# Softmax weights normalised by a product with diag(1/sum) on TensorE, in all attentions of a two-block transformer kernel

## The chip, the cores and the metric

The program runs on one core of a Trainium2 chip. The metric is the device time of one execution in microseconds (us); a kernel's figure is the median of its runs. A core has TensorE (PE in the rows, with PEld for its weight loads), VectorE (DVE), ScalarE (ACT), GpSimd (POOL) and SyncE (SP, which issues nearly all weight transfers here).

## The reference, cut to what matters

Two transformer blocks run after each other on 256 tokens of width 1024, all in float32. The first has two layers with a context stream beside the latent one, each layer with grouped attention, a Hyena convolution branch, a merge and a gated feed-forward. The second has one layer: a convolution branch and dilated attention, a memory cross-attention, and a mixture of 32 experts. Four kinds of attention occur, and all end in the same few lines:

```
s = jnp.einsum('bqhgd,bkhd->bhgqk', q_blk, keys) * scale
p = jax.nn.softmax(s, axis=-1)            # exp(s - max) / sum
out = jnp.einsum('bhgqk,bkhd->bqhgd', p, vals)
```

Before `p` can be multiplied with the values it must be divided by its row sums and turned, since TensorE sums over partitions: queries lie on the partitions of `p`, and keys must.

## The kernel before, in words

The kernel splits most float32 operands into a high part and a low part (`divide`: ScalarE writes the rounded high part, VectorE subtracts it for the low part) and multiplies them in three products (`mm3`). Weights come through `Stream`: SyncE loads pieces of 128x1024 into tiles `u`, the two halves are made from them, and the loads are issued some pieces ahead. Tiles `u` are 4 KB a partition, and there are NSLOT = 46 of them. Tiles `t` (2 KB, NTMP = 12) hold intermediate results; small columns are `s`; `ps` are the 8 banks that TensorE writes to.

The program's order is set as it is recorded, by a planner. Generators (projections, Hyena, attention) yield what they wait for; `drive` and `tick` step whichever can go on, by the estimates in `Timer`, which charges each instruction to its engine: for a TensorE product, n/2400 us times 4 for float32, or times 2 for a transposition, with a least of 0.107 us. Work whose operands are late by that estimate is put off by `defer`, and background work on VectorE (`modulation_sums`, products of 128x1024 with a column) is fed in between. All engines then run their queues in the recorded order. Each instruction is recorded through one helper, so nearly every row has line L289 (L290 in the changed kernel), and tiles must be told by name.

An attention of the first block goes by units of four heads: `scores` writes the scores of two heads to `ps`, `softmax` takes the row maximum on VectorE and the exponential on ScalarE, which leaves the row sums in `sm`. Its deferred `rest` takes the reciprocal, and multiplies the 128x512 or 128x256 exponentials in place by it (`times`: on ScalarE or VectorE, whichever the planner holds free first). Then `turn` transposes four heads at a time into one bank, a 128x128 block each, and `divide` splits what comes out. The other attentions have the same steps for pairs of 128x256: `softmax_pair`, where ScalarE does the multiplication, and `turn_probs`.

By units, layer 0 has 12 `turn` pairs of 4 blocks with 8 transpositions each, layer 1 has 8, the dilated attention 6, and the memory attention 4 groups of 4: 96 + 64 + 48 + 16 = 224 transpositions of exponentials. 112 other transpositions of `t` tiles stay as they are.

Two other places hold float32 products of the form that the change brings in. `leave` (the end of the memory attention) adds a residual 128x128 block of float32, as the stationary operand, times the identity `ident` into `acc`, by a plain `matmul` (not a transposition). And `route` begins with a loop over `range(self.WARM)`, WARM = 24, of plain products `ident` by `ident`.

Of the kernel before, what the change touches and what calls it, by code (L numbers as in the profile page):

```python
# [11 lines left out]
F32 = mybir.dt.float32  # L12
# [15 lines left out]
NE = 32  # L28
CAP = 32
EFF = 512  # L30
NSLOT = 46
NTMP = 12

# [160 lines left out]
class Part:  # L196
# [1 line left out]


    def __init__(self, ap, n=1):  # L200
        self.ap, self.left, self.eta = ap, n, None

    def __getitem__(self, key):
        return self.ap[key]
# [9 lines left out]
class Timer:  # L214
# [12 lines left out]
    def issue(self, engine, op, aps, kw):  # L227
        outs = [aps[0]] + ([kw["accum_out"]] if kw.get("accum_out") is not None else [])
        ins = aps[1:] + [v for k, v in kw.items() if k != "accum_out" and isinstance(v, bass.AP)]
        size = max(int(np.prod(a.shape[1:])) for a in aps)  # L230
        if op == "dma_start":
            engine = "DMA"
            start, cost = max(self.free["DMA"], self.free["PE"]), int(np.prod(aps[0].shape)) * 4 / 360e3
        else:
            start = self.free[engine]
            if engine == "PE":
                n = int(np.prod(aps[0].shape[1:]))
                slow = aps[-1].dtype == F32
                cost = n / 2400 * (2 if op == "transpose" else 4 if slow else 1)
                if "tile_position" in kw:  # L240
                    cost /= 4
                cost = max(cost, self.LEAST if slow else 0.03) + self.EACH
            else:
                cost = self.FIX[engine] + size * self.PER[engine]
        for a in ins:
            t, e = self.wrote.get(a.name, (0.0, engine))
            start = max(start, t + (self.LAG if e != engine else 0.0))
        for a in outs:
            t, e = self.wrote.get(a.name, (0.0, engine))
            if e != engine:  # L250
                start = max(start, t + self.LAG)
            t, e = self.read.get(a.name, (0.0, engine))
            if e != engine:
                start = max(start, t + self.LAG)
        end = start + cost
        self.free[engine] = end
        late = self.LATE if engine == "DMA" else 0.0
        for a in ins:
            if self.read.get(a.name, (0.0, engine))[0] <= end:
                self.read[a.name] = (end, engine)  # L260
        for a in outs:
            self.wrote[a.name] = (end + late, engine)

    def there(self, x):
        if isinstance(x, float):
            return x
        if isinstance(x, Part):
            if x.ready:
                return self.there(x.ap)
            return FAR if x.eta is None else x.eta  # L270
        if not isinstance(x, bass.AP):
            return x() if isinstance(x, types.FunctionType) else 0.0
        return self.wrote.get(x.name, (0.0, ""))[0] + self.LAG
# [145 lines left out]
class Net:  # L419
# [662 lines left out]
    def softmax(self, ps, n, scale):  # L1082

        nc = self.nc
        m, nb, sm, rs = ([self.small(1) for _ in ps] for _ in range(4))
        P = [Part(self.tmp()) for _ in ps]
        for i, p in enumerate(ps):
            nc.vector.tensor_reduce(m[i], p[:, :n], axis=AX, op=OP.max)
        for i, p in enumerate(ps):
            nc.vector.scalar_tensor_tensor(nb[i], m[i], -1.0, scale[i], op0=OP.mult, op1=OP.mult)  # L1090
        for i, p in enumerate(ps):
            nc.scalar.activation(P[i][:, :n], p[:, :n], AF.Exp, bias=nb[i], scale=scale[i], accum_out=sm[i])

        def rest(i):
            nc.vector.reciprocal(rs[i], sm[i])
            self.times(P[i][:, :n], P[i][:, :n], rs[i])
            P[i].done()
        for i in range(len(ps)):
            if not self.dry:
                P[i].eta = self.timer.there(sm[i]) + 0.8  # L1100
            self.defer(lambda i=i: rest(i), sm[i])
        return P

    def times(self, out, x, col):

# [6 lines left out]
    def attention(self, kT, V, Q, R, units):  # L1112

        nc = self.nc

        def scores(u, hs):
            g, i, k0, nk = u
            q = slice(i * 128, (i + 1) * 128)
            n = nk * 128
            ks = slice(k0 * 128, k0 * 128 + n)  # L1120
            ps = [self.ps() for _ in hs]
            for hh, p in zip(hs, ps):
                hd = 4 * g + hh
                self.need(Q[hd])
                self.need(kT[g])
                self.mm3(p[:, :n], Q[hd][:, 0, q], Q[hd][:, 1, q], kT[g][:, 0, ks], kT[g][:, 1, ks], True, True)
            return self.softmax(ps, n, [R[4 * g + hh][:, i:i + 1] for hh in hs])

        def turn(P, kt):
            ps = self.ps()  # L1130
            for hh in range(4):
                self.need(P[hh])
                self.transpose(ps[:, hh * 128:(hh + 1) * 128], P[hh][:, kt * 128:(kt + 1) * 128])
            o = Part(self.u([128, 2, 512], F32R))
            self.divide([(o[:, 0], o[:, 1], ps)], [o])
            return o

        def values(u, ps, part, kt):
            g, i, k0, nk = u
            gs = slice(g * 128, (g + 1) * 128)  # L1140
            v = V[k0 + kt]
            self.need(v)
            self.need(part)
            self.mm3(ps, v[:, 0, gs], v[:, 1, gs], part[:, 0], part[:, 1], kt == 0, kt == nk - 1)

        def finish(u, ps):
            g, i = u[:2]
            q = slice(i * 128, (i + 1) * 128)
            o = [Q[4 * g + hh] for hh in range(4)]
            self.divide([(o[hh][:, 0, q], o[hh][:, 1, q], ps[:, hh * 128:(hh + 1) * 128]) for hh in range(4)])  # L1150

        def score_steps(u, hs):
            g = u[0]
            while len(kT) <= g or any(4 * g + hh not in R or not self.known(Q[4 * g + hh]) for hh in hs) or \
                    not self.known(kT[g]):
                yield BLOCK
            yield (kT[g], *[x for hh in hs for x in (Q[4 * g + hh], R[4 * g + hh])])
            return scores(u, hs)

        last = None  # L1160
        for u in units + [None]:
            P = []
            if u:
                P += yield from score_steps(u, (0, 1))
            if last:
                v, PP = last
                yield PP
                PT = [turn(PP, kt) for kt in range(2)]
            if u:
                P += yield from score_steps(u, (2, 3))  # L1170
            if last:
                yield PT
                ps = self.ps()
                for kt in range(2):
                    values(v, ps, PT[kt], kt)
                if v[3] > 2:
                    PT = [turn(PP, kt) for kt in range(2, 4)]
                    yield PT
                    for kt in range(2, 4):
                        values(v, ps, PT[kt - 2], kt)  # L1180
                finish(v, ps)
            last = [u, P]
# [497 lines left out]

    def softmax_pair(self, ps, scale=None):

        nc = self.nc
        m, nb, sm, rs = (self.small(2) for _ in range(4))
        P = Part(self.tmps(SEQ)[0])
        if scale is None:
            nc.vector.tensor_reduce(nb, ps, axis=AX, op=OP.max, negate=True)
        else:
            nc.vector.tensor_reduce(m, ps, axis=AX, op=OP.max)
            nc.vector.scalar_tensor_tensor(nb, m, -1.0, scale, op0=OP.mult, op1=OP.mult)  # L1690
        for i in range(2):
            nc.scalar.activation(P[:, i], ps[:, i], AF.Exp, bias=nb[:, i:i + 1],
                                 scale=1.0 if scale is None else scale[:, i:i + 1],
                                 accum_out=sm[:, i:i + 1])

        def rest():
            nc.vector.reciprocal(rs, sm)
            for i in range(2):
                nc.scalar.activation(P[:, i], P[:, i], AF.Copy, scale=rs[:, i:i + 1])
            P.done()  # L1700
        if not self.dry:
            P.eta = self.timer.there(sm) + 0.8
        self.defer(rest, sm)
        return P

    def turn_probs(self, P, o=None):
# [2 lines left out]
        pt = self.ps().rearrange("p (k q) -> p k q", k=2)  # L1709
        for k in range(2):  # L1710
            for i in range(2):
                self.transpose(pt[:, k, i * 128:(i + 1) * 128], P[:, i, k * 128:(k + 1) * 128])
        if o is not None:
            self.nc.scalar.activation(o, pt, AF.Copy)
            return Part(o, 0)
# [701 lines left out]
```

## Time and profile before

| | |
|---|---|
| median of 3 runs | 2033.67 us (2031.07 to 2033.98) |
| profiled execution | 2032.56 us, of it 2030.8 us span from the first instruction to the last |
| mean granted TensorE clock | 0.987 |
| TensorE busy | 1914.3 us, 94% of the span |
| VectorE, ScalarE busy | 1080.7 us (53%), 711.9 us (35%) |

Busy time is an average over stages. By stretches of 50 us TensorE is busy for 45 us or more until about 1550 us, mostly 49 to 50; from about 1600 us on, in the experts, it is busy for 42 to 46 us and waits for weights, while the DMA engines move 407 to 409 GB/s. A matmul row's duration counts from its start to its modelled end, and these overlap; the cost of one in a dense stretch is the distance between starts. A plain float32 product leaves two records in the trace and two weight loads, a transposition one of each.

### The profile page before, as it was taken

The numbers are of one execution on the slowest core, as the hardware profiler recorded it, in microseconds if no ns is written. First come the engines' busy times: TensorE is split into PE (matmuls) and PEld (weight loads), VectorE is DVE, ScalarE is ACT, GpSimd is POOL, SyncE is SP. The second block draws the span as 40 slices with busy tenths as digits, with TensorE's granted clock in tenths as the row PEclk, the third lists the DMA queues.
The fourth block names the chain that finished last, engine by engine and source line by source line (L and its number), as shares of the span: only waits on it lengthen the run. The fifth ranks groups of instructions, "written<-read, shape, count | busy, mean of one in ns | idle before, by whom it ended". The sixth has DMA issues, their size and how long they took to land. (4 is left out here: it accounts for less than half of the span.)

```text
span 2030.8 us, 27948 instructions
## 1 busy us (share of the span) xinstructions
PE 1914.3 (94%) x11155; PEld 1444.2 (71%) x11155; DVE 1080.7 (53%) x1747; ACT 711.9 (35%) x1164; POOL 41.4 (2%) x49
## 2 busy tenths in 40 slices
PE   7999999999999999999999999999999898888886
PEld 3788888887878888899889999998888431111111
DVE  6988997376763343588877655578564210000001
ACT  3433664244322222364654544346652100000001
POOL 0000000000000000000000000000100000000000
PEclk9999999999999999999999999999999999999998
DMA  9434145443553242455267465553378999999997
GB/s 373 171 113 130 57 127 175 147 134 99 158 156 104 83 125 73 150 172 162 89 237 275 159 188 177 181 164 93 114 245 313 405 407 409 409 409 409 409 410 301
DMA packets 121437, 432.10 MB, mean 213 GB/s; under 512 B 13654, under 2 KB 14152, under 8 KB 121304
## 3 DMA queue, kind: packets, MB, share of 16 engines
q1 hardware_dynamic: 119464, 424.64, 58.8%
q0 software_dynamic: 1696, 5.38, 0.9%
q8 instruction: 89, 1.46, 0.3%
q14 instruction: 44, 0.36, 0.1%
q10 hardware_dynamic: 144, 0.26, 0.0%
HBM read 428.13 MB, written 2.10 MB: 212 GB/s over the span
## 5 line engine op out<-in xcount | busy, mean ns | idle before, releaser
L289 PE MATMUL ps<-u 128*128 128x256 f32 (+3 forms) x9088 | 1583.7, 346 | 46.5 <-DVE u L289 20.8
L289 PEld LDWEIGHTS ps<-u 128*128 128x128 f32 (+2 forms) x9088 | 1291.7, 187 | 329.3 <-DMA u<-w 105.2
L289 DVE TENSOR_TENSOR u<-u 128x1024 fp32r<-128x1024 f32 (+4 forms) x414 | 432.2, 1071 | 208.3 <-ACT u L289 197.0
L289 ACT ACTIVATE u<-u 128x1024 fp32r<-128x1024 f32 (+2 forms) x392 | 359.7, 961 | 269.7 <-DVE u L289 176.8
L289 PE MATMUL ps<-u,t 128*32 128x512 f32 (+1 forms) x1028 | 213.4, 618 | 33.3 <-DMA u<-w 21.1
L289 PEld LDWEIGHTS ps<-u,t 128*32 128x32 f32 (+1 forms) x1028 | 43.7, 111 | 186.5 <-DMA u<-w 115.7
L289 ACT ACTIVATE u<-ps 128x512 fp32r<-128x512 f32 (+3 forms) x201 | 88.8, 496 | 221.8 <-PE ps L289 220.2
L289 DVE TENSOR_TENSOR t<-t,ps 128x512 f32<-128x512 f32 x12 | 8.2, 686 | 255.2 <-PE ps L289 240.1
L289 DVE SCALAR_TENSOR_TENSOR u<-u,cs 128x1024 f32<-128x1024 f32 x112 | 139.9, 1278 | 0.1
L289 ACT ACTIVATE t<-ps 128x512 f32<-128x512 f32 (+1 forms) x62 | 36.5, 596 | 279.5 <-PE ps L289 279.3
L289 DVE TENSOR_TENSOR u<-u,ps 128x512 f32<-128x512 f32 x53 | 36.2, 686 | 101.4 <-PE ps L289 101.4
L289 DVE SCALAR_TENSOR_TENSOR u<-ps,mod,u 128x256 f32<-128x256 f32 x96 | 41.9, 478 | 72.8 <-PE ps L289 72.8
L289 DVE SCALAR_TENSOR_TENSOR u<-ps,s,u 128x512 fp32r<-128x512 f32 (+2 forms) x24 | 15.4, 662 | 115.9 <-ACT u L289 96.1
L289 ACT ACTIVATE u<-t 128x512 fp32r<-128x512 f32 (+1 forms) x74 | 41.8, 592 | 89.8 <-DVE t L289 84.4
L289 DVE TENSOR_TENSOR u<-ps,u 128x512 fp32r<-128x512 f32 (+2 forms) x135 | 59.4, 489 | 23.2 <-ACT u L289 16.3
L289 ACT ACTIVATE u<-ps,s 128x512 fp32r<-128x512 f32 (+1 forms) x26 | 15.9, 646 | 152.6 <-PE ps L289 149.0
L289 POOL TENSOR_TENSOR s<-s,mhalf 128x4 f32<-128x4 f32 (+2 forms) x25 | 30.2, 1206 | 1687.6 <-DVE s L289 1679.5
L289 ACT ACTIVATE t<-ps,s 128x256 f32<-128x256 f32 (+1 forms) x80 | 49.2, 629 | 40.6 <-DVE s L289 40.5
L289 PE MATMUL ps<-ident,t 128*128 128x128 f32 (+1 forms) x352 | 50.5, 278 | 9.3 <-DVE t L289 7.2
L289 PEld LDWEIGHTS ps<-ident,t 128*128 128x128 f32 (+1 forms) x352 | 40.3, 143 | 24.0 <-DVE t L289 14.7
L289 ACT ACTIVATE t<-u 128x512 f32<-128x512 f32 x41 | 25.3, 629 | 77.1 <-DVE u L289 76.8
L289 DVE TENSOR_TENSOR u<-t,u 128x512 fp32r<-128x512 f32 (+1 forms) x74 | 44.2, 642 | 2.6 <-ACT u L289 2.6
(132 smaller groups left out, 688.3 us busy)
## 6 DMA issues: line engine op xcount, KB each, us to landing
u<-w SPq DMA_DIRECT2D x381, 512.0 KB, 10.2
u<-w_in SPq DMA_DIRECT2D x102, 512.0 KB, 4.1
u<-w_mod SPq DMA_DIRECT2D x96, 512.0 KB, 4.8
u<-w_gu SPq DMA_DIRECT2D x88, 512.0 KB, 3.7
u<-w_dn SPq DMA_DIRECT2D x32, 512.0 KB, 3.6
u<-w_out SPq DMA_DIRECT2D x24, 512.0 KB, 4.4
u<-w_oa SPq DMA_DIRECT2D x16, 512.0 KB, 4.8
u<-w_dn SPq DMA_DIRECT2D x16, 384.0 KB, 3.2
```

Of the source, the lines that this page charges most:

```text
L289: return fn(*args, **kw)
```

## The change

The multiplication of the exponentials is dropped. `rest` builds instead a diagonal matrix `dg` of 128x128 from the identity times the reciprocal column (`diagonal`, by `times`, so on ScalarE or VectorE), and `turn` and `turn_probs` multiply: the exponentials are the stationary operand as before, but the moving one is the diagonal in place of the identity, and the instruction is a plain float32 matmul in place of a transposition. The eight `dg` tiles of 512 B take the room of one `u` tile: NSLOT goes from 46 to 45. In the planner, a TensorE product of 128 columns is charged like a transposition (times 2), and an attention weight counts as there once its diagonals are.

```
-NSLOT = 46
+NSLOT = 45
+NDIAG = 8
...
-                cost = n / 2400 * (2 if op == "transpose" else 4 if slow else 1)
+                cost = n / 2400 * (2 if op == "transpose" or n == 128 else 4 if slow else 1)
...
         def rest(i):
             nc.vector.reciprocal(rs[i], sm[i])
-            self.times(P[i][:, :n], P[i][:, :n], rs[i])
+            P[i].scales.append(self.diagonal(rs[i]))
             P[i].done()
...
+    def diagonal(self, col):
+        d = self.wp.tile([128, 128], F32, name="dg", tag="dg", bufs=NDIAG)
+        self.times(d, self.ident, col)
+        return d
...
-                self.transpose(ps[:, hh * 128:(hh + 1) * 128], P[hh][:, kt * 128:(kt + 1) * 128])
+                self.nc.tensor.matmul(ps[:, hh * 128:(hh + 1) * 128], P[hh][:, kt * 128:(kt + 1) * 128],
+                                      P[hh].scales[0], start=True, stop=True)
...
-            for i in range(2):
-                nc.scalar.activation(P[:, i], P[:, i], AF.Copy, scale=rs[:, i:i + 1])
+            P.scales += [self.diagonal(rs[:, i:i + 1]) for i in range(2)]
...
-                self.transpose(pt[:, k, i * 128:(i + 1) * 128], P[:, i, k * 128:(k + 1) * 128])
+                self.nc.tensor.matmul(pt[:, k, i * 128:(i + 1) * 128], P[:, i, k * 128:(k + 1) * 128], P.scales[i],
+                                      start=True, stop=True)
```

On TensorE, in the attention of layer 0 (`ps<-ident,t` are transpositions of exponentials, `ps<-u` products of split operands, `ps<-ones_87,t` row sums), there stands before:

```order
L289 MATMUL ps<-ident,t 128x128 x8
L289 MATMUL ps<-u 128x512 x6
L289 MATMUL ps<-ones_87,t 128x1 x8
L289 MATMUL ps<-u 128x512 x30
L289 MATMUL ps<-ident,t 128x128 x8
L289 MATMUL ps<-u 128x512 x30
L289 MATMUL ps<-u 128x256 x6
```

And now, at the same place (`ps<-dg,t` are the products with a diagonal):

```order
L290 MATMUL ps<-dg,t 128x128 x8
L290 MATMUL ps<-ones_87,t 128x1 x8
L290 MATMUL ps<-u 128x512 x36
L290 MATMUL ps<-dg,t 128x128 x8
L290 MATMUL ps<-u 128x512 x30
L290 MATMUL ps<-ones_87,t 128x1 x8
L290 MATMUL ps<-u 128x512 x24
L290 MATMUL ps<-u 128x256 x6
```

Each group of 8 transpositions has become 8 products at nearly the same place among the same work; row sums move by 6 to 24 products. Over the whole program 224 instructions change so, and the number of matmul instructions of each other form stays the same.

On ScalarE, at the start of the dilated attention (`t,s<-ps,s` are exponentials, `t<-t,s` their multiplication), there stands before:

```order
L289 ACTIVATE t,s<-ps,s 128x256 x4
L289 ACTIVATE u<-ps,s 128x256 x2
L289 ACTIVATE t<-t,s 128x256 x4
L289 ACTIVATE t,s<-ps,s 128x256 x4
L289 ACTIVATE t<-t,s 128x256 x4
L289 ACTIVATE u<-u 128x1024
L289 ACTIVATE u<-ps 128x512 x2
```

And now:

```order
L290 ACTIVATE t,s<-ps,s 128x256 x4
L290 ACTIVATE u<-ps,s 128x256 x2
L290 ACTIVATE t,s<-ps,s 128x256 x4
L290 ACTIVATE dg<-ident,s 128x128 x2
L290 ACTIVATE u<-ps 128x512 x2
L290 ACTIVATE u<-u 128x1024 x2
```

Of eight multiplications here, two diagonals stay on ScalarE and six go to VectorE. Over the program, 50 multiplications on ScalarE and 30 on VectorE become 22 diagonals on ScalarE and 58 on VectorE, and ScalarE switches its function table 20 times where it did 18 times.

## Rows read from the trace of the kernel before

**Rows 1.** Page, part 1: busy us of each engine, share, instructions.
```profile
PE 1914.3 (94%) x11155; PEld 1444.2 (71%) x11155; DVE 1080.7 (53%) x1747; ACT 711.9 (35%) x1164; POOL 41.4 (2%) x49
```
**Rows 2.** Stretches of the four attentions: length, then busy us, clock, DMA share, GB/s.
```profile
215.00:340.00 125.00, 124.45 (x645) 103.51 (x644) 112.32 (x246) 79.82 (x174) 3.28 (x2) 1.00 0.41 129
986.00:1056.00 70.00, 65.13 (x464) 59.27 (x462) 55.75 (x114) 46.39 (x90) 2.02 (x2) 1.00 0.44 145
1372.00:1452.00 80.00, 75.47 (x563) 64.34 (x563) 60.50 (x126) 56.24 (x132) 2.25 (x2) 0.98 0.29 91
1500.00:1530.00 30.00, 27.27 (x216) 26.86 (x215) 18.29 (x28) 19.27 (x40) 0.00 (x0) 0.94 0.72 248
```
**Rows 3.** Timeline of PE, layer 0: start us, duration, what, records.
```profile
248.97 7.77 PE L289 MATMUL ps<-u 128*128 128x512 f32 x36
256.58 1.03 PE L289 MATMUL ps<-ident,t 128*128 128x128 f32 x8
257.37 9.15 PE L289 MATMUL ps<-u 128*128 128x256 f32 x42
```
**Rows 4.** Timeline of PE at the end of the memory attention.
```profile
1540.93 1.14 PE L289 MATMUL ps<-ident,u 128*128 128x128 f32 x8
1541.90 0.98 PE L289 MATMUL ps<-t,u 128*128 128x36 f32 x8
...
1551.23 0.95 PE L289 MATMUL ps<-ones,acc 128*128 128x1 f32 x8
1552.04 4.55 PE L289 MATMUL ps<-u 128*128 128x256 f32 x36
```
**Rows 5.** The loop of WARM products on PE: records, busy us, mean ns.
```profile
L289 PE MATMUL ps<-ident 128*128 128x128 f32 x48 | 7.0, 317 | 0.0
```
**Rows 6.** Timeline of PE, memory attention: one group of four transpositions.
```profile
1505.03 0.60 PE L289 MATMUL ps<-ident,t 128*128 128x128 f32 x4
1505.38 6.00 PE L289 MATMUL ps<-u 128*128 128x256 f32 x48
```
**Rows 7.** Groups on DVE and ACT by form: busy us, mean ns, idle before.
```profile
L289 DVE TENSOR_TENSOR u<-ps,u 128x128 fp32r<-128x128 f32 x64 | 14.0, 281 | 1.7 <-ACT u L289 1.7
L289 DVE TENSOR_SCALAR t<-t,s 128x512 f32<-128x512 f32 x19 | 9.3, 487 | 0.7
L289 DVE TENSOR_SCALAR t<-t,s 128x256 f32<-128x256 f32 x14 | 4.9, 354 | 1.2 <-POOL s L289 0.8
...
L289 ACT ACT_TABLE_LOAD x18 | 23.1, 1283 | 4.9 <-DMA cols<-cols 4.6
L289 ACT ACTIVATE t<-t,s 128x256 f32<-128x256 f32 x37 | 16.8, 524 | 3.2 <-DVE s L289 3.2
L289 ACT ACTIVATE t<-t,s 128x512 f32<-128x512 f32 x13 | 9.4, 726 | 4.6 <-DVE s L289 4.6
L289 ACT ACTIVATE identr<-ident 128x128 fp32r<-128x128 f32 x1 | 0.3, 292 | 0.0
```
**Rows 8.** Waits of PE, layer 1, then dilated attention: us in total, times, longest.
```profile
PE ps L289 <- DVE u L289: 5.5, 3, 2.4
...
PE ps L289 <- ACT t L289: 4.1, 4, 1.6
```
**Rows 9.** Timeline, dilated attention: two waits of PE and what ScalarE did.
```profile
1405.53 0.73 PE L289 MATMUL ps<-u,identr 128*128 128x512 f32 x2 [1.62 <-ACT t L289]
...
1440.45 0.93 ACT L289 ACTIVATE t<-t,s 128x256 f32<-128x256 f32 x2
1441.04 0.94 PE L289 MATMUL ps<-ident,t 128*128 128x128 f32 x4 [0.96 <-ACT t L289]
```
**Rows 10.** SP's waits, 1450 to 1600 us; then a stretch of the experts, as rows 2.
```profile
SPq L289 <- PE ps L289: 75.2, 33, 14.7
...
1950.00:2000.00 50.00, 42.98 (x166) 8.99 (x166) 2.19 (x3) 1.97 (x3) 0.00 (x0) 1.00 1.03 409
```
**Rows 11.** Costliest group of VectorE's background products.
```profile
L289 DVE SCALAR_TENSOR_TENSOR u<-u,cs 128x1024 f32<-128x1024 f32 x112 | 139.9, 1278 | 0.1
```

More of the change, by code (lines that the diff above doesn't have):

```diff
@@ L200, in __init__ @@
     def __init__(self, ap, n=1):
-        self.ap, self.left, self.eta = ap, n, None
+        self.ap, self.left, self.eta, self.scales = ap, n, None, []
     def __getitem__(self, key):
@@ L268, in there @@
             if x.ready:
-                return self.there(x.ap)
+                return max(map(self.there, [x.ap, *x.scales]))
             return FAR if x.eta is None else x.eta
@@ L1102, in softmax @@
         return P
+    def diagonal(self, col):
+        if self.dry:
+            return None
+        d = self.wp.tile([128, 128], F32, name="dg", tag="dg", bufs=NDIAG)
+        self.times(d, self.ident, col)
+        return d
     def times(self, out, x, col):
```

## The prediction

> **What bounds the kernel now.** I read the page's busy shares first. TensorE is busy for 94% of the span, VectorE for 53%, ScalarE for 35% [rows 1]; the reader is to see that no other engine comes near. A share is a mean over stages, so next I cut out the four stretches with attention in them [rows 2]. In layer 0 TensorE is busy for 124.45 of 125 us at a granted clock of 1.00; in layer 1 for 65.13 of 70; in the dilated attention for 75.47 of 80; in the memory attention for 27.27 of 30. It idles there for 0.55 + 4.87 + 4.53 + 2.73 = 12.7 us in all. VectorE has 12.7 us of its own to spare in layer 0, ScalarE 45.2. So TensorE is the bound in all four, almost without slack in the first. Busy is not the same as dense, since the rows overlap; distances between starts tell. In layer 0, 36 split products of 512 columns and 8 transpositions follow each other without a gap: 7.61 us from start to start for the 36, or 0.211 each [rows 3]. TensorE runs as tightly as it does anywhere, and what is added to it there is added to the time.
>
> Whether a delay before the experts reaches the end is the second question. The experts are bound by transfers at 409 GB/s with the DMA engines' share at 1.03 [rows 10]. But those transfers start when buffers come free: between 1450 and 1600 us SyncE waits 75.2 us for TensorE to release tiles [rows 10]. All attentions lie ahead of it, so a TensorE that is later by X lets the stream start later by X.
>
> **The change on TensorE.** 224 transpositions become 224 plain float32 products of the same size: 96 in layer 0, 64 in layer 1, 48 in the dilated attention (26 groups of 8 together) and 16 in the memory attention (4 groups of 4).
>
> A group of 8 transpositions takes 257.37 - 256.58 = 0.79 us, 0.099 each [rows 3]; a group of 4 takes 0.35 [rows 6].
>
> The new form has a twin in the trace. A plain float32 product of a 128x128 block with 128 columns of the identity stands at the end of the memory attention: 8 records from 1540.93 to 1541.90, 0.97 us [rows 4]. Those are 4 products, for a plain float32 product leaves two records and two weight loads: the WARM loop of 24 products has 48 [rows 5]. So one costs 0.243 us against 0.099. As a lower bound I take float32 products with one column, which have almost nothing to stream: 8 records, 4 products, from 1551.23 to 1552.04, 0.81 us or 0.203 each [rows 4]. I take 0.243, since it is the same form; the lower bound stays for the range.
>
> A group of 8 then takes 1.94 us, 1.15 more than now; a group of 4 takes 0.97, 0.62 more. Layer 0: 12 x 1.15 = 13.8 us. Layer 1: 8 x 1.15 = 9.2. Dilated: 6 x 1.15 = 6.9. Memory: 4 x 0.62 = 2.5. Sum: 32.4 us. By the lower bound a group of 8 takes 0.83 more and one of 4 takes 0.46 more: 26 x 0.83 + 4 x 0.46 = 23.4 us.
>
> The rows thus show the plain product at 2.4 times the transposition. The Trainium skill says the same without a figure: its page "Perfetto Trace Analysis", section "Transposes", wants a logical transposition done as a transposition and not as a standard matmul, because the transposing form skips the arithmetic; the trace agrees, with 0.243 against 0.099 us. Its page "FP8 and Floating Point Precision", section "TensorE Precision Notes", gives a true float32 product four passes through the array; with the 53.3 ns for 128 columns at 2.4 GHz of the page "TensorE: Matmul & The Clock Gate", that makes an estimate of 0.213 us a product, and the sum by it would be 224 x 0.213 less the 21.9 us of the transpositions now, 25.8 us in place of 32.4.
>
> The planner charges the new product 0.107 us, like the transposition. That changes the order but no duration: groups stand where they stood, among the same products. TensorE will be later than the planner thinks, which makes operands early rather than late.
>
> **The change on ScalarE and VectorE.** ScalarE loses 50 multiplications, 16.8 + 9.4 = 26.2 us [rows 7], and gains 22 diagonals, at 0.292 us by the one copy of 128x128 from SBUF [rows 7]: 6.4 us. VectorE loses 19 of 0.487 and 11 of 0.354 us, 13.1 us, and gains 58 diagonals. A 128x128 scaling does not show on VectorE; below, it can't cost less than nothing; above, the 128x128 subtraction from PSUM takes 0.281 [rows 7]. I take the upper end, to which it is nearest in size: 16.3 us, 3 us more than before, spread over four stages with more than that to spare. Two more loads of ScalarE's table at 1.283 us [rows 7] lie on an engine that is free for a third of layer 0; if that cover fails they cost 2.6 us.
>
> So ScalarE is relieved by about 17 us net, and where does TensorE wait for it? In the dilated attention, 4.1 us in all [rows 8]. One wait of 0.96 us ends on a pair of multiplications: they run from 1440.45 for 0.93 us, and the transposition starts at 1441.04 once the first is done [rows 9]. The longest, 1.62 us, ends before a product with the mask, ahead of the softmax [rows 9]: it waits for a bank to be read by an exponential, and the change doesn't touch it. In layer 1 TensorE waits 5.5 us for VectorE [rows 8], for low parts of weights and not for a softmax.
>
> **What hides.** Part of the 12.7 us of idle time goes, because the relieved ScalarE is earlier or because the slower TensorE gives VectorE time. At the least nothing is hidden; at the most all 12.7. But VectorE's queue also holds row maxima that wait for TensorE's scores, and then the delay is passed on through it rather than hidden. I take half, 6.4 us, none of it in layer 0, where there is 0.55 to hide in.
>
> **The smaller pool.** One tile `u` less is one piece of 512 KB less in flight before the experts. At 409 GB/s [rows 10] that is 1.28 us if the stream is bound by tiles as it starts, and nothing if not. I take 0.6.
>
> **Sum.** 32.4 - 6.4 + 0.6 = 26.6 us on the profiled execution's 2032.56 (span 2030.8 and 1.8 around it): 2059.2. That execution lies 1.1 us below the median of the runs and within their spread, so I predict **2059 us**, 1.2% slower.
>
> **The rivals.**
> 1. *The slack swallows more.* All idle time in layer 1, dilated and memory attention goes: 32.4 - 12.7 + 0.6 = 20.3, 2053 us. For it: three of the four stretches have idle time of the size of what is added. Against it: the largest waits end on work that has nothing to do with the softmax. With the lower bound of a product as well, 23.4 - 12.7 = 10.7: 2043 us, the lowest end.
> 2. *The product costs no more than a transposition (faster).* The planner's new charge says so. Then nothing is added on TensorE, and the 4.1 us of waits on ScalarE in the dilated attention [rows 8] and half of the memory attention's 2.73 idle may go, 5.5 us: 2027 us. The point from which it decides: at a product of about 0.123 us the 224 extra costs equal those 5.5 us. Against it: two records and two loads for each plain product, and no row with one under 0.2 us at full clock.
> 3. *The diagonals come late.* 58 of 80 stand on VectorE now, where 30 multiplications did, and there they can stand behind a background product of 1.278 us [rows 11]. If the 20 groups of both layers each waited for one, that would add 25.6 us: 2085 us. Against it: the recorded order has the diagonals right behind their reciprocals, as the multiplications were, and other products of TensorE lie between exponentials and turn.
> 4. *Nothing is hidden.* 32.4 + 1.3 + 2.6 = 36.3: 2069 us.
>
> **How the numbers follow.** A measurement of this kernel can tell about 0.2%, 4 us, from no change. The forecast with its neighbours between 2053 and 2066 holds 0.60; rival 1, from 2043 to 2053, 0.20; rival 4, 2066 to 2072, 0.07; rival 3, above that, 0.06; rival 2, faster by over 0.2%, 0.04; within 0.2%, where a cheap product and little hiding meet, 0.03. Faster 0.04, same 0.03, slower 0.93. The range runs from rival 1's low end to a little above rival 4: 2043 to 2070.
>
> **What would show it.** In the profile of the changed kernel, groups of 16 records `ps<-dg,t` with about 1.9 us from their start to the next start: right; about 0.8: rival 2. Layer 0's attention longer by 12 to 14 us at an unchanged busy share of nearly 1. In layer 1 and the dilated attention a smaller idle time, 12.1 us down to about 6; if it rises, and the waits end on VectorE's `dg`, rival 3. The stretch of the experts as long as now, but later. The prediction fails if the groups are short, or if layer 0 grows by much less than 12 us.

## The result, and the profile after

The changed kernel takes 2052.37 us (median; 2050.44 to 2056.24) against 2033.56 before: a ratio of 1.0095, 95% interval 1.0083 to 1.0107. It is slower by 18.8 us; 26.6 had been forecast, and the time lies in the forecast range, 6.6 us below the predicted 2059. Its profiled execution has a span of 2048.7 us, 17.9 more than before.

Busy shares of the changed kernel (the page, part 1), against [rows 1]:

```profile
PE 1936.2 (95%) x11379; PEld 1463.8 (71%) x11379; DVE 1085.4 (53%) x1775; ACT 701.5 (34%) x1138; POOL 42.3 (2%) x49
```

TensorE has 224 records more and is busy 21.9 us longer. Its idle time falls from 2030.8 - 1914.3 = 116.5 to 112.5 us. What is new, by form (busy us, mean ns):

```profile
L290 PE MATMUL ps<-dg,t 128*128 128x128 f32 x448 | 55.5, 276 | 0.8 <-DVE dg L290 0.6
...
L290 ACT ACTIVATE dg<-ident,s 128x128 f32<-128x128 f32 x22 | 8.7, 406 | 6.0 <-DVE s L290 5.4
...
L290 DVE TENSOR_SCALAR dg<-ident,s 128x128 f32<-128x128 f32 x58 | 16.1, 286 | 1.8
```

448 records are 224 products with two each, as the loop of WARM products had said [rows 5]. What one costs is read from starts. Timeline of TensorE, layer 0 and memory attention of the changed kernel, against [rows 3, 4, 6]:

```profile
215.53 1.95 PE L290 MATMUL ps<-dg,t 128*128 128x128 f32 x16
217.34 1.95 PE L290 MATMUL ps<-ones,t 128*128 128x1 f32 x16
...
244.05 1.95 PE L290 MATMUL ps<-dg,t 128*128 128x128 f32 x16
245.75 7.78 PE L290 MATMUL ps<-u 128*128 128x256 f32 x36
...
1530.25 1.06 PE L290 MATMUL ps<-dg,t 128*128 128x128 f32 x8
1531.06 5.51 PE L290 MATMUL ps<-u 128*128 128x256 f32 x44
```

A group of 8 takes 1.70 us (244.05 to 245.75), 0.213 each, where split products follow, and 1.81 where other float32 products follow. Forecast was 1.94. A group of 4 takes 0.81 here and up to 0.91 elsewhere, against a forecast of 0.97. So each product more lengthens a group by (1.70 - 0.81) / 4 = 0.223 us, and a group that split products follow is a little shorter than its products would add up to.

Where the time came in shows at fixed points, products that stand at the same place in both programs: the norms (`ident,s`) and the last row sums (`ones,acc`). Before, then after:

```profile
120.39 0.60 PE L289 MATMUL ps<-ident,s 128*128 128x128 f32 x4
427.40 0.38 PE L289 MATMUL ps<-ident,s 128*128 128x128 f32 x2
477.60 0.62 PE L289 MATMUL ps<-ident,s 128*128 128x128 f32 x4
855.08 0.94 PE L289 MATMUL ps<-ones,acc 128*128 128x1 f32 x8
1138.11 0.38 PE L289 MATMUL ps<-ident,s 128*128 128x128 f32 x2
1348.65 0.60 PE L289 MATMUL ps<-ident,s 128*128 128x128 f32 x4
1551.23 0.95 PE L289 MATMUL ps<-ones,acc 128*128 128x1 f32 x8
```

```profile
120.37 0.60 PE L290 MATMUL ps<-ident,s 128*128 128x128 f32 x4
437.37 0.38 PE L290 MATMUL ps<-ident,s 128*128 128x128 f32 x2
487.51 0.62 PE L290 MATMUL ps<-ident,s 128*128 128x128 f32 x4
867.64 0.95 PE L290 MATMUL ps<-ones,acc 128*128 128x1 f32 x8
1155.33 0.38 PE L290 MATMUL ps<-ident,s 128*128 128x128 f32 x2
1365.95 0.60 PE L290 MATMUL ps<-ident,s 128*128 128x128 f32 x4
1569.43 0.73 PE L290 MATMUL ps<-ones,acc 128*128 128x1 f32 x6
```

From differences of these starts, in us, one profiled execution for each column (the last four columns are experiments told below, by the same points):

| stretch | before | changed | product with identity | transposed again | pool of 45 | pairs by free engine |
|---|---|---|---|---|---|---|
| layer 0 to its second norm | 307.0 | 317.0 | 316.9 | 309.8 | 306.9 | 307.1 |
| its feed-forward | 377.5 | 380.1 | 377.0 | 379.9 | 380.2 | 377.2 |
| layer 1 to its second norm | 283.0 | 287.7 | 290.1 | 279.2 | 283.6 | 283.0 |
| dilated and memory attention | 202.6 | 203.5 | 201.7 | 203.8 | 203.8 | 200.2 |
| from there to the end | 479.6 | 479.3 | 479.1 | 481.2 | 481.5 | 479.9 |

So +10.0 in layer 0's attention, +2.6 in a feed-forward that the change does not touch, +4.7 in layer 1, +0.9 in the last two attentions, and nothing in the experts. The three terms of the sum to be tested are the product, the pool, and what is hidden or relieved. A fourth, which the sum does not have, is the granted clock; it follows below.

What is hidden or relieved shows in TensorE's idle time. The stretches of [rows 2] in the changed kernel, shifted with the work (length, busy us of PE, PEld, DVE, ACT, POOL, clock, DMA share, GB/s):

```profile
215.00:360.00 145.00, 145.00 (x785) 123.22 (x784) 114.99 (x248) 80.55 (x173) 3.28 (x2) 1.00 0.37 120
997.00:1070.00 73.00, 69.10 (x489) 63.45 (x490) 56.72 (x119) 42.78 (x86) 2.92 (x2) 0.98 0.40 134
1385.00:1475.00 90.00, 87.48 (x683) 77.41 (x682) 74.91 (x154) 56.17 (x126) 2.24 (x2) 1.00 0.34 105
1515.00:1550.00 35.00, 33.37 (x273) 32.52 (x273) 21.57 (x38) 19.22 (x38) 0.00 (x0) 1.00 0.72 243
```

Idle were 12.7 us; now 0 + 3.9 + 2.52 + 1.63 = 8.0, in windows that are 38 us longer. In the dilated attention ScalarE's part of the waits is down from 4.1 [rows 8] to 1.7:

```profile
PE ps L290 <- ACT t L290: 1.7, 2, 1.1
```

One wait on a diagonal is new, in the memory attention:

```profile
1544.28 1.13 PE L290 MATMUL ps<-dg,t 128*128 128x128 f32 x8 [0.56 <-DVE dg L290]
```

Between fixed points the stretches can be compared as they are. Layer 1, then dilated and memory attention, before, in the changed kernel, and for the last stretch in the experiment with the identity told below (columns as in [rows 2]):

```profile
855.08:1138.11 283.03, 272.73 (x2080) 259.82 (x2079) 227.49 (x364) 150.52 (x245) 9.13 (x8) 0.98 0.56 188
1348.65:1551.23 202.58, 193.14 (x1507) 180.69 (x1505) 134.93 (x242) 107.27 (x217) 9.51 (x13) 0.97 0.53 174
...
867.64:1155.33 287.69, 278.20 (x2143) 265.31 (x2142) 227.07 (x366) 149.28 (x243) 10.03 (x8) 0.99 0.54 185
1365.95:1569.43 203.48, 197.16 (x1571) 186.04 (x1570) 140.59 (x264) 98.24 (x195) 9.45 (x13) 0.98 0.52 171
...
1365.07:1566.79 201.72, 195.37 (x1571) 184.58 (x1569) 135.06 (x242) 107.19 (x217) 9.16 (x13) 0.99 0.52 175
```

TensorE's idle time falls from 10.3 to 9.5 us in layer 1 and from 9.4 to 6.3 in the last two attentions. The granted clock differs too. Before, it stood at 0.50 for about 10 us of layer 1 (from 870, 901 and 1058 us) and for about 14 us of the last two attentions (from 1406, 1457, 1485 and 1519 us); in the changed kernel it did so for about 7 us each (from 913 and 1016, and from 1500). That is 10 us fewer at half clock; by these rows an estimate of up to 5 us of TensorE's time. Why it fell at these places was not tried. Three of these places before, and the longest in the changed kernel:

```profile
870.40:873.60 3.20, 3.20 (x15) 3.20 (x16) 3.20 (x6) 1.62 (x3) 0.00 (x0) 0.50 0.02 5
1406.30:1409.50 3.20, 3.20 (x14) 2.38 (x15) 1.64 (x4) 3.20 (x10) 0.00 (x0) 0.50 0.65 204
1457.50:1460.70 3.20, 3.20 (x17) 3.20 (x16) 3.20 (x6) 1.04 (x3) 1.36 (x2) 0.50 0.20 63
...
1500.50:1507.00 6.50, 6.45 (x30) 6.46 (x31) 6.50 (x12) 3.63 (x5) 1.62 (x1) 0.50 0.77 253
```

### The profile page after: what moved, and what is told of

It reads as the page before. It is cut to its first block, busy times and chain, and to the rows that moved or that the text cites. A ratio compares the mean times of both kernels' runs of the same rounds, so it can differ in the third digit from the quotient of the medians.

```text
span 2048.7 us, 28446 instructions
## 1 busy us (share of the span) xinstructions
PE 1936.2 (95%) x11379; PEld 1463.8 (71%) x11379; DVE 1085.4 (53%) x1775; ACT 701.5 (34%) x1138; POOL 42.3 (2%) x49
## 5 line engine op out<-in xcount | busy, mean ns | idle before, releaser
L290 PE MATMUL ps<-u,t 128*32 128x512 f32 (+1 forms) x1028 | 217.6, 611 | 30.1 <-DMA u<-w 21.4
L290 ACT ACTIVATE t<-ps 128x512 f32<-128x512 f32 (+1 forms) x62 | 36.3, 594 | 283.2 <-PE ps L290 283.0
L290 PE MATMUL ps<-dg,t 128*128 128x128 f32 x448 | 55.5, 276 | 0.8 <-DVE dg L290 0.6
L290 PEld LDWEIGHTS ps<-dg,t 128*128 128x128 f32 x448 | 53.5, 192 | 3.5 <-ACT u L290 1.1
```

The costliest lines, as they stand in the source:

```text
L290: return fn(*args, **kw)
```

## The experiments

Theory A: the length of the plain product is the cause. The others are named where they are told.

**The product alone.** The kernel before with nothing changed but the form of the 224 instructions (the planner's charge keeps the recorded order as it was):

```
-                self.transpose(ps[...], P[hh][...])
+                self.nc.tensor.matmul(ps[...], P[hh][...], self.ident, start=True, stop=True)
...
-                self.transpose(pt[...], P[...])
+                self.nc.tensor.matmul(pt[...], P[...], self.ident, start=True, stop=True)
...
-                cost = n / 2400 * (2 if op == "transpose" else 4 if slow else 1)
+                cost = n / 2400 * (2 if op == "transpose" or n == 128 else 4 if slow else 1)
```

> The kernel before in its recorded order, pool of 46 and multiplications unchanged; only the 224 transpositions are done as plain float32 products with the identity. Nothing but the length of the product is left of the change. Theory A: 224 x (0.213 - 0.099) = 25.5 us more work on TensorE, of which waits in layer 1, the dilated and the memory attention take up 5 to 9: 2050 to 2054 us, layer 0's norm 10 to 11 us later than the 427.4 of before, and the feed-forward behind it no longer than before (377.5 us), since the pool is whole. Theory B (order, diagonals and pool are the cause): under 2043 us.

Measured: 2052.4 us against 2034.34, ratio 1.0094, 1.0077 to 1.0111. That is the whole slowdown of the change, from the instruction's form alone: the order of instructions on TensorE, ScalarE and VectorE is the same in both traces. (The profile, and so the table's column, is of an execution of 2047.7 us, 4.7 below the median, so its stretches add up to 15.1 us more than before and not to 18.) Its timeline in layer 0, and layer 0's second norm:

```profile
250.53 1.95 PE L289 MATMUL ps<-ident,t 128*128 128x128 f32 x16
252.23 7.77 PE L289 MATMUL ps<-u 128*128 128x512 f32 x36
...
437.25 0.38 PE L289 MATMUL ps<-ident,s 128*128 128x128 f32 x2
```

The group of 8 takes 1.70 us here too, though its moving operand is the identity, and the norm comes 9.85 us later than before, almost as in the changed kernel. The feed-forward (377.0 us) does not get longer. Theory B is out. Layer 1 pays 7.1 us here against 4.7 in the change. The 2.4 us between them are idle time of TensorE, 12.0 us here and 9.5 there; whether the shorter diagonals or the other order gave them back was not tried apart.

**Products back to transpositions.** The changed kernel, diagonals built but not multiplied with:

```
-                self.nc.tensor.matmul(ps[...], P[hh][...], P[hh].scales[0], start=True, stop=True)
+                self.transpose(ps[...], P[hh][...])
```

(and so in `turn_probs`).

> The changed kernel with its 80 diagonals still built, but the 224 products done as transpositions with the identity again, in the same recorded order; the weights are left undivided by their sums. Theory A (the length of the plain product is the cause): TensorE loses 224 x (0.213 - 0.099) = 25.5 us of work, a part of which comes back as waits, so 2028 to 2035 us, at or below the 2033.6 of before, and layer 0's norm (437.4 us in the changed kernel, 427.4 before) falls back to about 427. Theory B (the diagonals and the new order are the cause): the time stays above 2043.

Measured: 2034.88 us against 2033.83, ratio 1.0011, 1.0001 to 1.0021. The change falls back by 17.5 us, so the product's price is confirmed from the other side. But the rest of the change is not a gain: it is a loss of 1 to 2 us. Layer 0 came back to 309.8, not 307.0, so the norm is 430.2 and not the 427 expected. Of these 2.8 us 1.1 are idle time, in new waits for ScalarE's tiles `t`; the others go with a stretch at half clock that the profile of before does not have there:

```profile
219.70:222.90 3.20, 3.20 (x9) 2.43 (x9) 3.20 (x10) 2.11 (x5) 1.58 (x1) 0.50 0.00 0
```

Layer 1 is 3.8 us shorter than before (279.2), but it stands at half clock once, from 906 us, where the profile of before does so three times, and only 0.4 us less of it is idle; so little of that is shown to be the new order. And 2.4 us are paid in the feed-forward.

**The pool.** The kernel before with one tile less:

```
-NSLOT = 46
+NSLOT = 45
```

> The kernel before with 45 tiles u in place of 46 and nothing else. If the experts' stream is bound by tiles as it starts, the end comes up to 1.3 us later (2033.6 to 2035) and the stretch from the last WARM product to the end grows by about 1 us, as between the two traces; if not, the stretch stays as it is and the 1 us there came from the order.

Measured: 2038.33 against 2033.45, ratio 1.0017, 1.0008 to 1.0026. The ratio is 3.5 us, more than the 1.3 that had been the upper bound, and it is not only at the experts (481.5 against 479.6 in one profile): the feed-forward of layer 0 takes 380.2 us for 377.5. (The profile is of an execution of 2040.45 us; 1.6 us of what it has over the kernel before lie ahead of the first fixed point, with a stretch at half clock from 38 us.) There a product that sums the modulation waits. Timeline of TensorE before, with the pool of 45, and in the changed kernel:

```profile
587.20 1.78 PE L289 MATMUL ps<-u,ones 128*32 128x512 f32 x8
```

```profile
592.06 1.05 PE L289 MATMUL ps<-u,ones 128*32 128x512 f32 x4 [2.58 <-DVE u L289]
```

```profile
600.46 1.05 PE L290 MATMUL ps<-u,ones 128*32 128x512 f32 x4 [2.58 <-DVE u L290]
```

The same wait of 2.58 us stands in the two kernels that share only the pool. What set it off shows in SyncE's waits from 478 to 600 us, before and with 45 tiles:

```profile
SPq L289 <- DVE u L289: 63.5, 17, 20.2
SPq L289 <- PE ps L289: 40.8, 10, 8.0
```

```profile
SPq L289 <- PE ps L289: 84.1, 17, 25.7
SPq L289 <- DVE u L289: 27.1, 11, 6.2
```

With one tile less, the tile that a transfer gets is more often one that TensorE frees: SyncE waits 84.1 us for TensorE where it waited 40.8, and its longest wait is 25.7 us where it was 20.2. VectorE's background sums, which need those pieces, then end late for TensorE. That the late piece is the one the sums waited for is read from these waits, not tried apart.

**By halves.** Diagonals and products in the first block alone (`softmax` and `turn` changed, the pairs as before), and in the pairs alone:

```
-            P.scales += [self.diagonal(rs[:, i:i + 1]) for i in range(2)]
+            for i in range(2):
+                nc.scalar.activation(P[:, i], P[:, i], AF.Copy, scale=rs[:, i:i + 1])
```

(with `transpose` again in `turn_probs`; the other half likewise, in `softmax` and `turn`).

> Diagonals and products in the two layers of the first block alone (160 products), multiplication and transposition as before in the dilated and memory attentions. Theory A, with the shifts of the landmarks between the two traces: +10 in layer 0's attention, +2.6 in its feed-forward, +4.7 in layer 1, so 2050 to 2052 us. Theory C (each product costs its share of the 18.8 us): 160/224 of it, +13.4, 2047 us.

Measured: 2052.67, ratio 1.0093, 1.0078 to 1.0108, as the landmarks had it within 1 us and not the 2047 of shares.

> Diagonals and products in the dilated and memory attentions alone (64 products), the first block as before. Theory A with slack: their 7.3 us of work are met by waits that go; the dilated attention comes out about 0.5 us shorter, the memory attention 1.5 longer: 2033 to 2036 us, no change that can be measured. Theory C: 64/224 of 18.8, +5.4, 2039 us.

Measured: 2040.1, ratio 1.0034, 1.0022 to 1.0046. The time of theory C, 2039, but not for its reason. The two halves add up to 25 us where the whole has 18.8. Each has the pool of 45, which accounts for 3.5 of the 6.3 us between them; the rest is open. In this profile the first block, whose instructions are those of before, loses 6 us in its feed-forward (860.98 - 477.50 = 383.5): the wait of 2.58, and from its end on a stretch at half clock:

```profile
590.96 1.92 PE L290 MATMUL ps<-u,ones 128*32 128x512 f32 x4 [2.58 <-DVE u L290]
...
592.00:596.00 4.00, 4.00 (x12) 2.52 (x9) 0.00 (x0) 0.60 (x2) 0.00 (x0) 0.50 0.58 187
596.00:600.00 4.00, 4.00 (x19) 3.26 (x18) 2.29 (x4) 1.03 (x1) 0.00 (x0) 0.85 0.27 63
```

The granted clock is 0.50 from 592 to 596 us and 1.00 again from 600. The same wait in the profiles of the other five kernels with 45 tiles was not followed by it. How many executions it befalls is open. Theory A had left the pool out of this kernel; its 3.5 us are most of the 4.1 by which the median passes the range.

**The planner's charge.** The changed kernel with `or n == 128` taken out, so that a product is charged 0.213 us:

```
-                cost = n / 2400 * (2 if op == "transpose" or n == 128 else 4 if slow else 1)
+                cost = n / 2400 * (2 if op == "transpose" else 4 if slow else 1)
```

> The changed kernel, but its planner charges a plain float32 product of 128 columns 0.213 us, what the trace shows, in place of 0.107. Theory A: the order hardly matters, 2050 to 2054 us. Theory D (the undercharged product spoils the plan): the new waits, 2.6 us in layer 0's feed-forward and 0.6 on a diagonal in the memory attention, go, 2048 to 2050 us.

Measured: 2056.39, ratio 1.0110, 1.0094 to 1.0125: not better than the change, if anything worse, and theory D falls. Theory A missed its upper end by 2.4 us; in the profile layer 1 takes 291.5 us (869.7 to 1161.1 us) for 287.7, and TensorE waits 10.1 us for VectorE's tiles `u` there, for 8.0 in the changed kernel; the other 1.7 us go with one stretch more at half clock, from 1083 us. An honest charge does not make a better order here.

**The relief without the product.** The kernel before, where only the pairs' multiplication may go to either engine:

```
             for i in range(2):
-                nc.scalar.activation(P[:, i], P[:, i], AF.Copy, scale=rs[:, i:i + 1])
+                self.times(P[:, i], P[:, i], rs[:, i:i + 1])
```

> The kernel before, no diagonals; only the multiplication of the pairs (dilated and memory attention) may go to VectorE or ScalarE, whichever the planner holds free first, as the diagonals may. If the waits that went in the dilated attention went because ScalarE was relieved, they go here too, without the longer products: 2 to 4 us less, 2030 to 2032 us. If they went because TensorE was slower there, nothing changes: 2033 to 2035.

Measured: 2029.39 us against 2033.45, ratio 0.9975, 0.9965 to 0.9985. It beats both kernels, and lies 0.6 us below what had been expected at best. Dilated and memory attention together take 200.2 us for 202.6, and in the same stretch of work TensorE waits 4.4 us for tiles `t` of ScalarE where it waited 6.3 before:

```profile
PE ps L289 <- ACT t L289: 4.4, 3, 2.2
```

```profile
PE ps L289 <- ACT t L289: 6.3, 5, 2.2
```

TensorE's idle time there is 8.1 us for 9.4; the other half of the 2.4 us goes with 10 us at half clock for 14. So to free the choice of engine is a gain that can be had by itself. It does not show that this is what shortened the waits of the changed kernel, 3.9 us in the same stretch. In the experiment with the identity ScalarE keeps all its multiplications, the order is that of before, and the wait falls as far:

```profile
PE ps L289 <- ACT t L289: 3.4, 3, 2.2
```

There the idle time is 6.4 us, as in the changed kernel (6.3). The longer products alone give ScalarE that time, so the relief by the diagonals is not shown in the changed kernel.

## Why the prediction was right, and where its sizes were off

- *TensorE bounds the attentions, and what is added there comes through to the end*: right. Layer 0's attention grew by 10.0 us with TensorE busy for all 145 of 145 us, and no stretch behind made up for it. From the last row sums to the end it takes 479.3 us where it took 479.6: later, not longer.
- *224 plain products for 224 transpositions, two records each*: right, by the records, and by the two experiments that change nothing but the form, from either side (+18 and -17.5 us).
- *0.243 us a product* was too much, and with it the term of 32.4 us. It measured 0.213 (1.70 us for 8). The twin's 0.97 us for 4 [rows 4] ran up to a further float32 product, and holds 0.08 us beyond four times 0.223; a share of that edge was counted with each product, and so twice in a group of 8. The changed kernel shows the lengthening too, 1.81 for 8 where float32 row sums follow, but 17 of the 20 groups of 8 in the two layers are followed by split products and take 1.70 us (one 1.81), and the six of the dilated attention take 1.71 to 1.98. At 0.91 more for each group of 8 and 0.50 for one of 4, the term is 26 x 0.91 + 4 x 0.50 = 25.7 us, a little more with the six. In layer 0 it is 12 x 0.91 = 10.9, and 10.0 came out, with 0.55 us of idle time gone. The estimate that the prediction worked out from the Trainium skill ("FP8 and Floating Point Precision", section "TensorE Precision Notes": a true float32 product takes four passes through the array) had been 0.213 us a product and 25.8 in all. The groups of 8 agree with it at 0.213; each product more costs 0.223, 5% above it.
- *6.4 us hidden*: the size was too small, and a part of it is a term that the prediction had put at nothing, the granted clock. 25.7 us of products and 2.6 of the pool's wait came out as 17.9, so 10.4 us were taken off. Of these 0.55 + 0.8 + 3.1 = 4.5 us are idle time that went in layer 0, in layer 1 and in the last two attentions. Some 5 us are the estimate for the 10 us fewer at half clock in the same places. TensorE's idle time fell by 2.3 us in the experts as well, but that stretch is only 0.3 us shorter. The relief of ScalarE, which the prediction gave as one reason, is not needed for it: the products with the identity have the same idle time in the last two attentions.
- *The sum* came near partly by luck: 6.7 us too many for the products, 4.0 too few hidden and 2.0 too few for the pool make the 8.7 us between 26.6 and 17.9, and the clock, which no term had, is in it.
- *The smaller pool, 0.6 us at the experts*: the term that was wrong in kind. It costs 2 to 5 us, and 2.7 of them stand in the feed-forward of layer 0, by a wait of 2.58 us that is in all six profiles here with 45 tiles and in none of the three with 46. The prediction looked for the price of a tile where transfers bind, and passed over the stretch where SyncE waits for tiles to come free and background sums have a date.
- *Rival 1 (the slack swallows more)* gave 2053 and the median is 2052.4, but not by its mechanism: 8.0 of the 12.7 us of idle time are still there. A cheaper product, a dearer pool and less time at half clock meet at its number. (It subtracts 12.7 us for three stretches that have 12.1.)
- *Rival 2 (the product costs no more)* is out by the products' rows, *rival 3 (late diagonals)* too: only one wait of 0.56 us ends on a diagonal. The 58 diagonals on VectorE take 0.286 us each, next to the 0.281 assumed; the 22 on ScalarE 0.406, more than the 0.292 of the copy. *Rival 4 (nothing is hidden)* is out by the idle time that went.

## What to carry to other kernels

An instruction that does two jobs at once is no gain where it runs on the engine that bounds: here the scaling had lain beside TensorE for almost nothing, and was put into instructions of twice the length on it. Where the trace holds a twin of the new instruction, read it in the neighbourhood that the new one will have, since what follows it belongs to the distance. When two profiles are compared stage by stage, the granted clock of each stage belongs beside its length: here one stretch at half clock more or less moved a stage by 1 to 3 us, as much as the smaller effects looked for. And a buffer taken from a shared pool is to be priced at every stretch where a transfer waits for one, not only where transfers bind.

## What the runs showed of the hardware that was not expected

A plain float32 product of 128x128 by 128 columns costs 0.213 us in a group of 8 that split products follow, whatever its moving operand holds (identity or diagonal), 2.15 times the 0.099 of the float32 transposition there. Each product more costs 0.223 us, twice the 0.11 of a transposition more, (0.79 - 0.35) / 4. The same wait of 2.58 us was followed by some microseconds at half clock in one profile (0.50 from 592 to 596 us) and by none in five others. And the kernel whose TensorE has more to do, and waits less, stood at half clock for a shorter time: its mean granted clock is 0.992 in the profile, where it was 0.987 before.
